# Summing one conditioning vector by TensorE instead of GpSimd, and a wider spacing of the conditioning loads between the first FFN's output weights

## Chip, core and metric

One core of one Trainium2 chip runs the whole program. The metric is device time in microseconds (us). Five engines work in order, each on its own queue: TensorE (PE, matmuls; its weight loads are listed as PEld), VectorE (DVE), ScalarE (ACT), GpSimd (POOL) and SyncE (SP), which here only issues DMAs. They wait for each other by semaphores.

## What is computed

Two transformer layers on 512 tokens of width 1024, in fp32: layer 0 has a gated linear recurrence (HGRN2) as mixer, layer 1 dilated attention; each is followed by a SwiGLU FFN of width 2816. Every layer is conditioned by six vectors of 1024 (shift, scale and gate for mixer and FFN), all from one vector `c`:

```
cond = silu(c)
for layer in range(2):
    mod = cond @ ada_w[layer] + ada_b[layer]
    sh1, sc1, g1, sh2, sc2, g2 = split(mod, 6)
    u = rms_norm(h, norm_g[layer, 0]) * (1 + sc1) + sh1
    y = hgrn2_mixer(u) if layer == 0 else dilated_attention_mixer(u)
    h = h + (1 + g1) * rms_norm(y, norm_g[layer, 1])
    u = rms_norm(h, norm_g[layer, 2]) * (1 + sc2) + sh2
    y = (silu(u @ w_gate) * (u @ w_up)) @ w_out
    h = h + (1 + g2) * rms_norm(y, norm_g[layer, 3])
```

## The kernel before

**Weights.** All weights and all `ada_w` pieces come through one stream (`Stream`, lines 35 to 140): a list `items` in a fixed order, 1 MB or less each, loaded by SP into two buffers `raw` in turn (line 70; the two bias rows of a gate at line 64). A buffer is loaded again when its last reader has done. A weight item is split into two parts for three-pass fp32 matmuls: ACT writes `hi` (line 90), DVE writes `lo = raw - hi` (line 91), and each has three buffers. The helper `three` (lines 575 to 578) issues the three matmuls of a product, hi, lo and the low part of the other operand.

**Conditioning.** A vector (l, v) is made in two halves of 512 columns (hf), each from two loads of 512 rows of `ada_w` (kq). In `ada_chunk` DVE multiplies each 128-row block by its scalar of `cond` and adds it up in an accumulator of 128 x 512 (lines 391 and 393). What is left is the sum over the 128 partitions: for most vectors GpSimd does it (`partition_all_reduce`, line 395), and then `col_fin` turns it into columns with DVE, one masked reduction of 128 x 128 for each of four column blocks (line 405, two instructions each). For the three vectors (0, 2), (0, 3) and (0, 4) the products are made by TensorE (`ada_groups`), and the sum too: `col_fin` multiplies each 128-column block of the accumulator by a column of ones (line 420) into one PSUM bank of tag "b". Either way DVE then adds the bias (line 409) and, for scales, the norm's weight (line 411).

**Order.** `weave` (in `block_kernel`) puts conditioning items between the weights: group n of the others goes in behind weight number first + n * every. The vectors (0, 2), (0, 4), (0, 3) and (1, 4) are woven into the mixer's input weights; (0, 5), (1, 1) and (1, 0) into the first FFN's. Of the eleven output weights of that FFN (`f0b`, two 128-row blocks each), each is used for 48 matmuls of 128 x 512 into all eight PSUM banks; the last two are used together, token block by token block (`mm`), while the norm of the next layer (`Turn`: lines 605 to 680) already begins.

In the mixer (heads in `head_prep` and `core_a` to `core_d`, lines 1496 to 1596) and in the FFN's output products up to the last two weights, a scheduler orders each engine's instructions by estimated times; so the change moves instructions that it doesn't touch. A head's output is normalised with 1/rms by GpSimd (`orr`, line 591) from DVE's `rv` (line 590); DVE scales it into `aT` (line 1588), TensorE transposes that (line 1595), and ACT copies it out (line 1596). GpSimd also makes two decay-weighted copies of each head, `k` (line 1534) and `q` (line 1537).

Of the kernel before, what the change touches and what calls it, by code (L numbers as in the profile page):

```python
# [292 lines left out]
def block_kernel(tc, x, c, positions, ada_w, ada_b, norm_g, hgrn_w_in, lower, hgrn_norm_g, hgrn_w_out,  # L293
# [8 lines left out]
    with ExitStack() as ctx:  # L302
# [7 lines left out]
        def bank(tag):  # L310
            uid[0] += 1
            return psum.tile([P, 512], F32, name=f"ps_{tag}{uid[0]}", tag=tag, bufs={"mm": 4, "a": 2, "b": 2}[tag])

        def fresh(p, shape, tag, bufs=1, dt=F32):
            uid[0] += 1
            return p.tile(shape, dt, name=f"{tag}{uid[0]}", tag=tag, bufs=bufs)
# [39 lines left out]
        def acc_place():  # L356
            turns_of_acc[0] += 1
            return shared[:, 2 + turns_of_acc[0] % 2]

        by_pe = lambda l, v: l == 0 and v in (2, 3, 4)  # L360

        def ada_groups(l, v, hf, kq):


            def run(raw):
                if kq == 0:
                    accs[l, v, hf] = bank("mm")
                ps, r = accs[l, v, hf], V4(raw)
                for k in range(4):
                    j = slice(32 * k, 32 * k + 32)  # L370
                    pe.matmul(ps[j], cond_tiles[:, kq * 4 + k], r[:, k], start=kq == 0, stop=kq == 1,
                              tile_position=(0, 32 * k))
                if kq == 1:
                    accs[l, v, hf] = acc_place()
                    act.copy(accs[l, v, hf], ps)
            return run

        def ada_chunk(l, v, hf, kq):
            if by_pe(l, v):
                return ada_groups(l, v, hf, kq)  # L380

            def run(raw):
                if kq == 0:
                    accs[l, v, hf] = acc_place()
                a = accs[l, v, hf]
                r = V4(raw)
                for k in range(4):
                    kt = kq * 4 + k
                    sc = cond[:, kt:kt + 1]
                    if kt == 0:  # L390
                        dve.tensor_scalar(a, r[:, k], sc, None, op0=OP.mult)
                    else:
                        dve.scalar_tensor_tensor(a, r[:, k], sc, a, op0=OP.mult, op1=OP.add)
                if kq == 1:
                    pool.partition_all_reduce(a, a, P, bass.bass_isa.ReduceOp.add)
            return run

        def ada_item(l, v, hf, kq):
            src = ada_w[l, kq * 512:(kq + 1) * 512, v * D + hf * 512:v * D + (hf + 1) * 512]
            return ("ada", src.rearrange("(k p) n -> p k n", p=P), ada_chunk(l, v, hf, kq), (l, v, hf, kq))  # L400

        def to_col(dst, rows, k):

            jk = fresh(base, [P, P], "diag", 1)
            dve.tensor_tensor_reduce(jk, rows[:, k * P:(k + 1) * P], ident, 1.0, 0.0, OP.mult, OP.add, dst)

        def col_done(l, v, sl, src=None):
            dst = cols[:, l * 4 + v - (1 if v > 2 else 0), sl]
            dve.tensor_add(dst, dst if src is None else src, abc(l, v)[:, sl])
            if v in (1, 4):  # L410
                dve.scalar_tensor_tensor(dst, dst, 1.0, ngc(l, 0 if v == 1 else 2)[:, sl], op0=OP.add, op1=OP.mult)

        def col_fin(l, v, hf):

            def run(_=None):
                a = accs.pop((l, v, hf))
                if by_pe(l, v):
                    b = bank("b")
                    for k in range(4):
                        pe.matmul(b[:, k:k + 1], a[:, k * P:(k + 1) * P], ones[:, 0:1], start=True, stop=True)  # L420
                    col_done(l, v, slice(hf * 4, hf * 4 + 4), b[:, 0:4])
                    return
                for k in range(4):
                    c = l * 4 + v - (1 if v > 2 else 0)
                    to_col(cols[:, c, hf * 4 + k:hf * 4 + k + 1], a, k)
                col_done(l, v, slice(hf * 4, hf * 4 + 4))
            return run

        def row_fin(l, v, hf):

            def run(raw):
                if hf == 0:
                    gates[l, v] = fresh(base, [P, D], "gate", 1)
                g = gates[l, v][:, hf * 512:(hf + 1) * 512]
                a = accs.pop((l, v, hf))
                if by_pe(l, v):
                    b = bank("b")
                    pe.matmul(b, ones, a, start=True, stop=True)
                    a = b
                dve.tensor_add(g, a, raw[:, 0:512])  # L440
                dve.scalar_tensor_tensor(g, g, 1.0, raw[:, 512:D], op0=OP.add, op1=OP.mult)
            return run
# [9 lines left out]
        def ada_seq(*vecs):  # L452

            res, last = [], None
            for l, v in vecs:
                for hf in range(2):
                    res.append([ada_item(l, v, hf, 0)])
                    res.append(([fin_item(*last)] if last else []) + [ada_item(l, v, hf, 1)])
                    last = (l, v, hf)
            return res + [[], [fin_item(*last)]]  # L460
# [15 lines left out]
        def weave(ws, others, first, every=1):  # L476

            res, o, n = [], list(others), 0
            for i, w in enumerate(ws):
                res.append(w)  # L480
                while i >= first + n * every and o:
                    res += o.pop(0)
                    n += 1
            return res + [i for g in o for i in g]

        items = []
# [11 lines left out]
        def ffn_ws(l):  # L498

            a, w = [], ffn_w_in[l]  # L500
            for j in range(PLAIN[l]):
                a += [win(w, j * 256), win(w, DFF + j * 256)]
            for f in range(2 * PLAIN[l], NF):
                a.append(("quarters", tuple(w[:, c:c + P].rearrange("(k p) n -> p k n", p=P) for c in (DFF + f * P, f * P))))
            return a, [wrow(ffn_w_out[l], j) for j in range(NF // 2)]

        items += weave(hg, ada_seq((0, 2), (0, 4), (0, 3), (1, 4)), 1, 0.7) + hg_o
        f0a, f0b = ffn_ws(0)
        n0 = 2 * PLAIN[0]
        gate, gate_fins = ada_halves(0, 5)  # L510
        one, two = ada_seq((1, 1)), ada_seq((1, 0))
        items += weave(f0a[:n0], [one[0], one[1], [], one[3][:1]], 2) + f0a[n0:]
        late = [gate[0], gate[1], gate[2], gate_fins[:1] + gate[3], one[2], gate_fins[1:] + one[3][1:], two[0], one[5] + two[1]]
        items += weave(f0b, late + two[2:], 0, 0.8)
        AW = attn_w_in[0]

        def av(g, hf):
# [30 lines left out]
        late = ada_seq((1, 2), (1, 3))  # L548
# [785 lines left out]
        early, late = slice(0, 256), slice(256, S)  # L1334
# [1040 lines left out]
        for kind, g, i in order:  # L2375
            if kind == "v":
                steps += [("v", None, None, k, *p) for k, p in enumerate(value_unit(g - 1, i))]
            else:
                two = sevens(g, i) if by_seven(g) else plain(g, i)
# [120 lines left out]
```

## Time and profile before

| | |
|---|---|
| time, median of three runs | 1509.28 us (1507.06 to 1509.78) |
| the profiled execution's own time | 1508.73 us |
| its span, first to last instruction | 1507.0 us |
| TensorE: busy, mean granted clock | 98% of the span, 0.993 |
| busy share of DVE, ACT, POOL | 73%, 53%, 13% |
| mean DMA rate | 133 GB/s |
| mixer of layer 0, in this trace | about 90 to 300 us |
| output weights of the first FFN | about 540 to 686 us |

How to read the views: a row of the timeline gives start, duration, engine, line, operation, output<-inputs, and in brackets the idle time of the engine before it and what ended it. Matmuls overlap, so the spacing of their starts is what one costs. In a table by windows, the sixth entry is the granted TensorE clock as a share of the full one (PEclk). Rows of "SPq" are DMAs being issued.

### The profile page before, as it was taken

The page shows a single profiled execution, that of the slowest core. Times are in us where ns is not written, and L with a number is a line of the kernel's source. Part 1 is how long each engine was busy: PE and PEld are TensorE (multiplying, and loading weights), DVE is VectorE, ACT ScalarE, POOL GpSimd, SP SyncE. Part 2 cuts the span into 40 slices and gives each one's busy share as a digit, 9 for nine tenths or more (in the row PEclk, how much of TensorE's full clock was granted, in tenths as well). Part 3 has the DMA queues.
Part 4 walks back from the last instruction along what each step waited for, and adds up shares of the span by engine and source line. Part 5 has one row for each costly group of instructions (what it writes and reads, how often), then busy time and mean ns, then how long its engine had stood idle before and what let it go on. Part 6 is the DMA issues. An engine that isn't in the chain of part 4 may idle for free. (4 is left out here: it accounts for less than half of the span.)

```text
span 1507.0 us, 25055 instructions
## 1 busy us (share of the span) xinstructions
PE 1477.4 (98%) x9807; PEld 1323.1 (88%) x9807; DVE 1096.8 (73%) x1816; ACT 797.3 (53%) x1474; POOL 197.5 (13%) x174
## 2 busy tenths in 40 slices
PE   8999998999999999999999999999999999999998
PEld 6777787888999997788999999999988899999886
DVE  4577677578688876777788877878766978887533
ACT  4433342464455542256637878567875655555231
POOL 1011013031111110222001010001012211110100
PEclk9999999999999999999999999999999999999999
DMA  9554553315333345634234443254343333434531
GB/s 307 179 173 138 184 168 112 112 57 157 93 107 108 107 155 206 226 136 140 82 121 137 131 129 94 81 161 123 91 154 126 97 100 113 113 111 142 199 110 56
DMA packets 210151, 201.09 MB, mean 133 GB/s; under 512 B 8248, under 2 KB 167920, under 8 KB 209776
## 3 DMA queue, kind: packets, MB, share of 16 engines
q1 hardware_dynamic: 207056, 192.71, 40.7%
q10 hardware_dynamic: 1952, 6.65, 1.2%
q8 instruction: 77, 1.26, 0.3%
q0 software_dynamic: 1024, 0.13, 0.2%
q14 instruction: 42, 0.34, 0.1%
HBM read 192.31 MB, written 5.31 MB: 131 GB/s over the span
## 5 line engine op out<-in xcount | busy, mean ns | idle before, releaser
L91 DVE TENSOR_TENSOR lo<-raw,hi 128x2048 fp32r<-128x2048 f32 x43 | 103.2, 2402 | 62.5 <-ACT hi L90 62.4
L90 ACT CAST hi<-raw 128x2048 fp32r<-128x2048 f32 x43 | 82.1, 1909 | 123.6 <-DMA raw<-in_ffn_w_out_dram 51.9
L576 PE MATMUL ps_mm<-uh,hi 128*128 128x512 f32 (+1 forms) x400 | 146.2, 366 | 0.0
L577 PE MATMUL ps_mm<-ul,hi 128*128 128x512 f32 (+1 forms) x400 | 144.8, 362 | 1.0 <-DVE ul L676 1.0
L578 PE MATMUL ps_mm<-uh,lo 128*128 128x512 f32 (+1 forms) x400 | 144.2, 360 | 0.0
L1981 PE MATMUL ps_mm<-apart,hiq 128*128 128x256 f32 (+1 forms) x608 | 142.0, 326 | 0.1
L1981 PEld LDWEIGHTS ps_mm<-apart,hiq 128*128 128x128 f32 x608 | 99.9, 189 | 8.3 <-ACT xs L2095 0.3
L1981 PE MATMUL ps_mm<-apart,loq 128*128 128x256 f32 (+1 forms) x304 | 97.4, 320 | 0.4 <-DVE loq L2117 0.4
L963 PE MATMUL ps_mm<-tl,hiq 128*128 128x256 f32 x340 | 93.9, 276 | 0.0
L963 PE MATMUL ps_mm<-th,loq 128*128 128x256 f32 x340 | 93.9, 276 | 0.0
L963 PE MATMUL ps_mm<-th,hiq 128*128 128x256 f32 x340 | 93.9, 276 | 0.0
L954 DVE TENSOR_TENSOR loq<-raw,hiq 128x1024 fp32r<-128x1024 f32 x68 | 80.3, 1222 | 18.6 <-ACT hiq L950 18.6
L576 PEld LDWEIGHTS ps_mm<-uh,hi 128*128 128x128 f32 x400 | 75.5, 189 | 18.4 <-issue 6.7
L577 PEld LDWEIGHTS ps_mm<-ul,hi 128*128 128x128 f32 x400 | 75.7, 189 | 12.5 <-DVE ul L676 1.4
L578 PEld LDWEIGHTS ps_mm<-uh,lo 128*128 128x128 f32 x400 | 75.5, 189 | 12.6 <-issue 1.1
L576 PE MATMUL ps_mm<-hi,oh 128*128 128x512 f32 x208 | 82.3, 396 | 4.2 <-ACT hi L90 4.2
L934 POOL TENSOR_TENSOR raw<-raw 128x512 f32<-128x512 f32 x34 | 44.8, 1316 | 304.6 <-DVE spare L930 138.6
L577 PE MATMUL ps_mm<-lo,oh 128*128 128x512 f32 x208 | 81.4, 392 | 0.0
L950 ACT CAST hiq<-raw 128x1024 fp32r<-128x1024 f32 x68 | 68.1, 1049 | 17.5 <-DVE raw L938 15.9
L1981 PE MATMUL ps_mm<-uh,hiq 128*128 128x256 f32 x256 | 71.8, 281 | 0.0
L1981 PE MATMUL ps_mm<-ul,hiq 128*128 128x256 f32 x256 | 71.2, 278 | 0.0
L1981 PE MATMUL ps_mm<-uh,loq 128*128 128x256 f32 x256 | 71.2, 278 | 0.0
(479 smaller groups left out, 4636.4 us busy)
## 6 DMA issues: line engine op xcount, KB each, us to landing
raw<-in_ada_w_dram SPq DMA_DIRECT2D x40, 1024.0 KB, 5.0
raw<-in_ffn_w_in_dram SPq DMA_DIRECT2D x136, 256.0 KB, 4.0
raw<-in_ffn_w_out_dram SPq DMA_DIRECT2D x22, 1024.0 KB, 4.8
raw<-in_attn_w_in_dram SPq DMA_DIRECT2D x64, 256.0 KB, 4.6
raw<-in_hgrn_w_in_dram SPq DMA_DIRECT2D x12, 1024.0 KB, 5.3
raw<-in_attn_w_in_dram SPq DMA_DIRECT2D x12, 1024.0 KB, 4.9
raw<-in_ffn_w_in_dram SPq DMA_DIRECT2D x10, 1024.0 KB, 5.0
raw<-in_attn_w_in_dram SPq DMA_DIRECT2D x16, 512.0 KB, 4.9
```

Source lines behind the costliest of these rows:

```text
L90: self.nc.scalar.copy(hi, t)
L91: self.nc.vector.tensor_sub(lo, t, hi.bitcast(F32))
L576: pe.matmul(ps, ah, bh, start=start, stop=False, skip_group_check=part)
L577: pe.matmul(ps, ah, bl, start=False, stop=False, skip_group_check=part)
L578: pe.matmul(ps, al, bh, start=False, stop=stop, skip_group_check=part)
L934: pool.tensor_add(r[:, 2], r[:, 2], r[:, 0])
L950: act.copy(hi, src)
L954: dve.tensor_sub(lo, src, hi.bitcast(F32))
L963: pe.matmul(ps, w[x][:, a], us[kt][y], start=begin and kt + m == 0, stop=kt == 3 and m == 2, skip_group_check=True)
L1981: pe.matmul(dst(), x, y, start=begin and i == 0, stop=i == len(todo) - 1, skip_group_check=True)
```

## The change

A second predicate, `sum_by_pe`, is true for the three vectors that TensorE already made and for (1, 4), the scale of layer 1's FFN. It takes the place of `by_pe` where the sum over partitions is chosen: for (1, 4) GpSimd's `partition_all_reduce` isn't issued, and `col_fin` takes the branch with four matmuls against ones. The products of (1, 4) stay on DVE. And in the weave of the first FFN's output weights, `every` goes from 0.8 to 0.95.

```
-        by_pe = lambda l, v: l == 0 and v in (2, 3, 4)
+        by_pe = lambda l, v, hf: l == 0 and v in (2, 3, 4)
+        sum_by_pe = lambda l, v, hf: by_pe(l, v, hf) or (l, v) == (1, 4)
...
-            if by_pe(l, v):
+            if by_pe(l, v, hf):
                 return ada_groups(l, v, hf, kq)
...
-                if kq == 1:
+                if kq == 1 and not sum_by_pe(l, v, hf):
                     pool.partition_all_reduce(a, a, P, bass.bass_isa.ReduceOp.add)
...
                 a = accs.pop((l, v, hf))
-                if by_pe(l, v):
+                if sum_by_pe(l, v, hf):
                     b = bank("b")
                     for k in range(4):
                         pe.matmul(b[:, k:k + 1], a[:, k * P:(k + 1) * P], ones[:, 0:1], start=True, stop=True)
...
                 a = accs.pop((l, v, hf))
-                if by_pe(l, v):
+                if sum_by_pe(l, v, hf):
                     b = bank("b")
                     pe.matmul(b, ones, a, start=True, stop=True)
                     a = b
...
-        items += weave(f0b, late + two[2:], 0, 0.8)
+        items += weave(f0b, late + two[2:], 0, 0.95)
```

From line 361 on, a line of the changed kernel has a number higher by one.

On GpSimd, in the mixer, the rows before are these (ISA rows without operands switch the code that GpSimd runs):

```order
L591 TENSOR_TENSOR orr_1920<-rv_1921,expo 128x4
L395 ISA
L395 ISA shared<-shared 128x512
L1537 ISA
L1537 TENSOR_TENSOR q_2063<-qd_2041,fpre_2047 128x512
L591 TENSOR_TENSOR orr_1994<-rv_1995,expo 128x4
```

In the changed kernel the same place reads:

```order
L592 TENSOR_TENSOR orr_1920<-rv_1921,expo 128x4
L1538 TENSOR_TENSOR q_2063<-qd_2041,fpre_2047 128x512
L592 TENSOR_TENSOR orr_1994<-rv_1995,expo 128x4
L1535 TENSOR_TENSOR k_2173<-T_1902,fsuf_2157 128x512
L1538 TENSOR_TENSOR q_2172<-qd_2150,fpre_2156 128x512
```

The all-reduce and the two switches around it are gone; the same happens once more, two instructions later, for the second half of the vector.

On TensorE, in the same stretch, the transposes of a head (`aT_1988`) stand before the change between two triples of a gate's products (`ps_mm_2187`):

```order
L576 MATMUL ps_mm_2187<-uh,hi_1809 128x512
L577 MATMUL ps_mm_2187<-ul,hi_1809 128x512
L578 MATMUL ps_mm_2187<-uh,lo_1810 128x512
L1595 MATMUL ps_a_2027<-ident,aT_1988 128x128 x4
L576 MATMUL ps_mm_2187<-uh,hi_1809 128x512
```

In the changed kernel (that bank is `ps_mm_2179` there):

```order
L577 MATMUL ps_mm_2179<-uh,hi_1809 128x512
L421 MATMUL ps_b_2088<-ones,shared 128x1 x4
L1596 MATMUL ps_a_2027<-ident,aT_1988 128x128 x4
L578 MATMUL ps_mm_2179<-ul,hi_1809 128x512
```

The four transposes come eleven matmuls earlier, behind the first new group of four matmuls against ones. The second new group stands later, among the small products of the next head (line 1548).

On SP, in the first FFN's output weights, the loads from the sixth weight on stand so before (`ada_w` pieces, the two bias rows of a gate, and weights):

```order
L70 DMA raw_5318<-in_ada_w_dram 128x4x512
L64 DMA raw_5324<-in_ada_b_dram 128x512
L64 DMA raw_5324<-in_norm_g_dram 128x512
L70 DMA raw_5387<-in_ada_w_dram 128x4x512
L70 DMA raw_5391<-in_ffn_w_out_dram 128x2x1024
L70 DMA raw_5398<-in_ada_w_dram 128x4x512
L70 DMA raw_5404<-in_ffn_w_out_dram 128x2x1024
```

And in the changed kernel:

```order
L70 DMA raw_5310<-in_ada_w_dram 128x4x512
L70 DMA raw_5316<-in_ffn_w_out_dram 128x2x1024
L64 DMA raw_5378<-in_ada_b_dram 128x512
L64 DMA raw_5378<-in_norm_g_dram 128x512
L70 DMA raw_5385<-in_ada_w_dram 128x4x512
L70 DMA raw_5445<-in_ffn_w_out_dram 128x2x1024
L70 DMA raw_5452<-in_ada_w_dram 128x4x512
```

The sixth weight is loaded ahead of the bias rows and of one conditioning piece; from there to the end, one weight and one conditioning piece alternate, and the eleventh weight comes behind the last conditioning piece, where before it followed the tenth directly. With it TensorE's order changes in three of the weights (the sixth, seventh and eighth): before, the eight `hi` matmuls (seven in one case) of a weight's first block come ahead of all `lo` matmuls; in the changed kernel each bank takes its three matmuls in a row, so that `lo` is needed one matmul after `hi`.

More of the change, by code (lines that the diff above doesn't have):

```diff
@@ L358, in acc_place @@
             return shared[:, 2 + turns_of_acc[0] % 2]
-        by_pe = lambda l, v: l == 0 and v in (2, 3, 4)
+        by_pe = lambda l, v, hf: l == 0 and v in (2, 3, 4)
+        sum_by_pe = lambda l, v, hf: by_pe(l, v, hf) or (l, v) == (1, 4)
         def ada_groups(l, v, hf, kq):
@@ L378, in ada_chunk @@
         def ada_chunk(l, v, hf, kq):
-            if by_pe(l, v):
+            if by_pe(l, v, hf):
                 return ada_groups(l, v, hf, kq)
@@ L393, in run @@
                         dve.scalar_tensor_tensor(a, r[:, k], sc, a, op0=OP.mult, op1=OP.add)
-                if kq == 1:
+                if kq == 1 and not sum_by_pe(l, v, hf):
                     pool.partition_all_reduce(a, a, P, bass.bass_isa.ReduceOp.add)
@@ L416, in run @@
                 a = accs.pop((l, v, hf))
-                if by_pe(l, v):
+                if sum_by_pe(l, v, hf):
                     b = bank("b")
@@ L435, in run @@
                 a = accs.pop((l, v, hf))
-                if by_pe(l, v):
+                if sum_by_pe(l, v, hf):
                     b = bank("b")
@@ L513, in block_kernel @@
         late = [gate[0], gate[1], gate[2], gate_fins[:1] + gate[3], one[2], gate_fins[1:] + one[3][1:], two[0], one[5] + two[1]]
-        items += weave(f0b, late + two[2:], 0, 0.8)
+        items += weave(f0b, late + two[2:], 0, 0.95)
         AW = attn_w_in[0]
```

## Prediction

> **What bounds the kernel now.** I read the page's busy times first, then TensorE's waits, then the timeline around the two longest. The page:
>
> ```profile
> PE 1477.4 (98%) x9807; PEld 1323.1 (88%) x9807; DVE 1096.8 (73%) x1816; ACT 797.3 (53%) x1474; POOL 197.5 (13%) x174
> ```
>
> TensorE is busy for 98% of the span, so only its work and its pauses can change the time. Who it waited for (total, times, longest), the two longest of all:
>
> ```profile
> PE ps_a L1595 <- DVE aT L1588: 6.3, 2, 4.8
> PE ps_mm L576 <- ACT hi L90: 4.2, 1, 4.2
> ```
>
> The first lies in the mixer (place H). On TensorE's timeline:
>
> ```profile
> 245.32 0.39 PE L577 MATMUL ps_mm<-ul,hi 128*128 128x512 f32 x1
> 245.55 0.39 PE L578 MATMUL ps_mm<-uh,lo 128*128 128x512 f32 x1
> 250.69 0.71 PE L1595 MATMUL ps_a<-ident,aT 128*128 128x128 f32 x4 [4.76 <-DVE aT L1588]
> 251.08 0.75 PE L576 MATMUL ps_mm<-uh,hi 128*128 128x512 f32 x1
> 254.82 0.40 PE L576 MATMUL ps_mm<-uh,hi 128*128 128x512 f32 x1
> ```
>
> A 128x512 matmul costs 0.23 us, start to start. After the wait nine of them take 254.82 - 251.08 = 3.74 us, 0.42 each. The windows (sixth entry is the clock) say why, here and after the other wait:
>
> ```profile
> 251.00:255.00 4.00, 4.00 (x13) 3.21 (x12) 4.00 (x9) 0.69 (x1) 1.31 (x1) 0.57 0.00 0
> 604.00:609.00 5.00, 5.00 (x12) 3.48 (x13) 5.00 (x8) 0.22 (x1) 2.26 (x1) 0.50 0.77 227
> ```
>
> So a long wait is paid twice: idle, then some 4 to 5 us at about half the clock. Without the wait, 254.82 would be 245.55 + 0.23 + 0.39 (transposes) + 9 x 0.23 + 0.1 (change of operation) = 248.3: place H loses **6.5 us**.
>
> Who held it up is on GpSimd's and DVE's timelines:
>
> ```profile
> 237.39 3.25 POOL L395 PARTITION_ALL_REDUCE shared<-shared  x1 [7.64 <-DVE ki L1509]
> 247.76 1.04 POOL L1537 TENSOR_TENSOR q<-qd,fpre 128x512 f32<-128x512 f32 x1 [7.12 <-issue]
> 248.77 1.05 POOL L591 TENSOR_TENSOR orr<-rv,expo 128x4 f32<-128x4 f32 x1
> 249.85 0.69 DVE L1588 TENSOR_TENSOR aT<-ps_b,orr 128x512 f32<-128x512 f32 x1 [4.85 <-POOL orr L591]
> ```
>
> The transposes wait for `aT`, that for `orr`, and `orr` stands in GpSimd's queue behind the all-reduce of (1, 4). The all-reduce takes 3.25 us, but a pause of 7.64 us lies ahead of it and one of 7.12 us, in which nothing was waited for, behind it: the switches of code. It is these 14.8 us that hold the queue.
>
> The second wait (place F) is in the first FFN's output weights:
>
> ```profile
> 599.16 0.39 PE L578 MATMUL ps_b<-hi,ol 128*128 128x512 f32 x1
> 603.75 0.79 PE L576 MATMUL ps_mm<-hi,oh 128*128 128x512 f32 x1 [4.21 <-ACT hi L90]
> 609.89 0.40 PE L577 MATMUL ps_b<-lo,oh 128*128 128x512 f32 x1
> 588.66 0.34 SPq L64 DMA_DIRECT2D raw<-in_ada_b_dram  x1
> 594.17 0.38 SPq L70 DMA_DIRECT2D raw<-in_ada_w_dram  x1
> 594.83 0.38 SPq L70 DMA_DIRECT2D raw<-in_ffn_w_out_dram  x1
> 601.80 1.90 ACT L90 CAST hi<-raw 128x2048 fp32r<-128x2048 f32 x1 [7.26 <-DMA raw<-in_ffn_w_out_dram]
> ```
>
> From 599.16 to 609.89 are 15 starts, worth 3.4 us at 0.227: place F loses **7.3 us**. The sixth weight was issued only at 594.83; the buffer that came free at 588.66 went to the bias rows, and the next one to another conditioning piece.
>
> **The change at place H.** Added: two groups of four matmuls against ones. One such group stands in the trace already:
>
> ```profile
> 236.67 0.95 PE L420 MATMUL ps_b<-ones,shared 128*128 128x1 f32 x8
> 237.48 0.48 PE L576 MATMUL ps_mm<-uh,hi 128*128 128x512 f32 x1
> ```
>
> It takes 237.48 - 236.67 = 0.81 us of TensorE; two cost 1.6 us, and nothing hides them. Removed: both all-reduces with their switches, and DVE's 16 instructions of line 405, replaced by the bias add alone. Neither GpSimd's nor DVE's work counts by itself; what counts is when `aT` is ready. The rows for that:
>
> ```profile
> 233.52 3.34 DVE L1509 RECIPROCAL ki<-bb 128x512 f32<-128x512 f32 x1
> 240.67 0.29 DVE L405 CUSTOM_DVE_ANT_0 diag<-shared,ident 128x128 f32<-128x128 f32 x1 [3.81 <-POOL shared L395]
> 244.32 0.69 DVE L1511 TENSOR_TENSOR qd<-bb,Q 128x512 f32<-128x512 f32 x1
> 242.37 0.39 PE L576 MATMUL ps_mm<-uh,hi 128*128 128x512 f32 x1
> ```
>
> The reciprocal ends at 236.86, where DVE stood 3.81 us for the all-reduce. What lies between that and `aT` took until 244.32 + 0.69 = 245.0, 4.3 us; so in the changed kernel it ends by 241.2, and `aT` (0.69) by 241.9. `orr` isn't later: its `rv` stands among those DVE instructions, and GpSimd needs 1.04 + 1.05 us for `q` and `orr`. TensorE comes to the new group behind 22 matmuls from 237.48, at 242.37 + 0.23 = 242.6, and to the transposes 0.81 later. The margin is 0.7 us at the new group (its PSUM bank is one that `aT` reads) and 1.5 at the transposes: the wait goes, and the half clock with it. Net at H: 6.5 - 1.6 = **4.9 us**. If the cover of 0.7 us is gone, each us late costs one. The second group waits for the accumulator's last products. DVE has twelve instructions for it behind `aT`, up to 0.7 us each (about 6.7 us in all, an estimate from the rows above: 248.6); TensorE has the group, the transposes, 20 matmuls and four small products of the next head ahead of it, about 6.9 us from 242.6 (249.5): no wait, or a few tenths.
>
> The Trainium skill, GPSIMD Engine Reference, section 4.1 Engine selection, names GpSimd for reducing along the partition dimension, which speaks against this edit. By it the sum should stay on GpSimd, and H would gain nothing; the trace disagrees, with 0.81 us against 3.25 plus the switches.
>
> **The change at place F.** The sixth weight takes the buffer at 588.66. The rows that time what follows:
>
> ```profile
> 592.18 0.69 DVE L440 TENSOR_TENSOR gate<-shared,raw 128x512 f32<-128x512 f32 x1 [0.93 <-DMA raw<-in_ada_b_dram]
> 603.73 3.68 DVE L91 TENSOR_TENSOR lo<-raw,hi 128x2048 fp32r<-128x2048 f32 x1 [0.80 <-ACT hi L90]
> 614.63 2.29 DVE L91 TENSOR_TENSOR lo<-raw,hi 128x2048 fp32r<-128x2048 f32 x1 [1.12 <-ACT hi L90]
> 616.95 0.37 SPq L70 DMA_DIRECT2D raw<-in_ffn_w_out_dram  x1
> 625.95 0.37 SPq L70 DMA_DIRECT2D raw<-in_ffn_w_out_dram  x1
> 621.68 1.91 ACT L90 CAST hi<-raw 128x2048 fp32r<-128x2048 f32 x1 [3.45 <-DMA raw<-in_ffn_w_out_dram]
> 653.22 0.39 PE L577 MATMUL ps_mm<-lo,oh 128*128 128x512 f32 x1
> ```
>
> A weight lands 4.7 us after its issue (616.95 to 621.68), so the sixth is there by 594 and its `hi` by 596. Ahead of its `lo` DVE has to add the bias rows, now issued some 4 us later, at about 592.5; they need 3.5 us (588.66 to 592.18): 596.0, then 0.6 for the add and 2.3 for `lo`: 598.9. TensorE asks for it at 599.6. The 7.3 us go, but two smaller waits come, because the loads now run one buffer turn behind each other to the end. The seventh weight is issued beside a conditioning piece at 599.6, as 594.83 was beside 594.17, and takes the same 7.0 us: 606.6. `hi` to 608.5; `lo` lies beside an all-reduce, as the row of 3.68 us did, and takes about 3.4: 611.9, where TensorE wants it at 610.5. **Wait of 1.4 us.** Then each turn is 9.0 us (616.95 to 625.95): the `lo` of the eighth to eleventh weights at 620.9, 629.9, 639.0 and 648.0, give or take 0.3. TensorE takes 48 x 0.227 = 10.9 us a weight and gains on them, but the last two weights are used together: the eleventh's `lo` is wanted 13 matmuls into the tenth, at 599.4 + 1.4 + 4 x 10.9 + 2.9 = 647.3. **Wait of 0.9 us**, to 648.2. Before, that matmul started at 653.22 (the last row). Net at F: **5.0 us**, bounded by 7.3 if both new waits vanish, and by 0 if the chain of loads slips.
>
> **Sum.** 4.9 + 5.0 = 9.9 us; less a tenth for norm work that starts nearer to TensorE: 9.8. The profiled execution took 1508.73 us (span 1507.0); 1508.73 - 9.8 = **1498.9 us**. The median before is 0.55 above that execution; I leave it in the range. Everything later is TensorE-bound with waits of 1.3 us at most, so the gain isn't given back there.
>
> **Rivals.** *Both places clean*: 4.9 + 7.3, so 1496.5. For it: my 3.4 us for `lo` and 7.0 for the load come from pairs that may fall apart. *New waits cost clock too*:
>
> ```profile
> 151.86 0.85 PE L1595 MATMUL ps_a<-ident,aT 128*128 128x128 f32 x4 [1.56 <-DVE aT L1588]
> 152.00:156.00 4.00, 4.00 (x38) 3.64 (x38) 1.33 (x5) 0.69 (x1) 0.00 (x0) 0.57 0.76 281
> ```
>
> A wait of 1.56 us, behind a group against ones, was followed by 4 us at 0.57, so 1.7 us lost. If either new wait does that, 0.8 to 1.7 us go, 2.5 for both: about 1500.9. The Trainium skill (TensorE: Matmul & The Clock Gate, "What's actually happening") has the clock fall after an idle window of about 3.4 us. By that rule waits of 1.4 and 0.9 cost no clock and the sum stays; the row at 152 shows a fall after 1.56, so I keep the rival. *One place only*: 1508.73 - 4.9 = 1503.8 if the wait at F merely moves; 1505.3 if H keeps its wait and adds the 1.6. Against it: the margins above. *Slower*: the loads at F slip by one buffer turn, 9.0 us, say because the bias rows land late and the seventh weight with them. GpSimd's last all-reduce then ends nearer to the norm:
>
> ```profile
> 638.74 3.23 POOL L395 PARTITION_ALL_REDUCE shared<-shared  x1 [14.99 <-DVE shared L393]
> 656.94 0.60 POOL L627 TENSOR_TENSOR rr<-rv,expo 128x1 f32<-128x1 f32 x1 [14.97 <-DVE rv L625]
> 660.72 0.76 DVE L651 TENSOR_SCALAR xn<-h,rr 128x1024 f32<-128x1024 f32 x1 [0.67 <-POOL rr L627]
> 663.88 0.60 PE L657 MATMUL ps_mm<-ident,xn 128*128 128x128 f32 x4
> ```
>
> Before it ended at 641.97 with 15 us to spare for the switch of 7.1. By my times it ends at 646; a turn later, 655.1 + 7.1 = 662.2 for `rr`, which is 6.9 us ahead of the transposes at 663.88: 669.1, so 5.2 late, with two falls of the clock, 2.3 us each (H and F lost 1.6 and 3.0 beyond their idle time). 1508.73 - 4.9 + 5.2 + 4.6 = 1513.6. It decides only if the loads slip by about 6 us or more.
>
> **Chances.** Forecast 0.52, both clean 0.15, clock 0.16, one place 0.09, in between (two halves lost) 0.04, slower 0.04. The range, 1495.0 to 1504.5, takes in the first three and "one place" but for 1505.3, and 1.5 us at the low end for the spread of the runs (1507.06 to 1509.78). Over 0.2% (3 us, about what a measurement of this kernel can tell from no change) faster: the first four but 0.02 of "one place", 0.90; within: 0.06; slower: 0.04.
>
> **What would show it.** H is right if no wait stands ahead of line 1596, the clock there stays at 1, and GpSimd's `q` and `orr` follow `rv` at once. F is right if the sixth weight's `hi` starts near 594 (less the 4.9 of H), and TensorE waits only for `lo` of the seventh and of the eleventh weight. A wait for `ps_b` at line 421, or a clock below 1 after 611 or 648, would make it wrong.

## The result, and the profile after

The changed kernel takes 1503.27 us (median of 5 runs, 1500.42 to 1505.12) beside 1509.78 for the kernel before on the same chip: ratio 0.9952, 95% interval 0.9940 to 0.9964, so 7.2 us faster (5.4 to 9.1). Two repeats gave 0.9955 (0.9942 to 0.9968) and 0.9962 (0.9948 to 0.9976): 6.8 and 5.7 us. The prediction said 9.8 us: right in its sign and its range, 2.6 to 4 us too much in size.

The profiled execution took 1504.35 us (span 1502.6). Its page, and TensorE's longest waits (total, times, longest):

```profile
PE 1476.8 (98%) x9823; PEld 1323.5 (88%) x9823; DVE 1095.8 (73%) x1800; ACT 797.2 (53%) x1474; POOL 191.3 (13%) x172
```

```profile
PE ps_a L2321 <- ACT h L2306: 2.7, 1, 2.7
PE ps_mm L578 <- DVE lo L91: 2.4, 2, 1.8
PE ps_a L1596 <- DVE aT L1589: 1.6, 1, 1.6
```

Both waits that the prediction started from are gone. Two waits for `lo` in the FFN's output weights are new, and the longest now stands at line 2321, the end of attention, where 0.7 us stood before.

**Place H** on the timeline of the changed kernel, GpSimd, DVE and TensorE:

```profile
236.90 1.01 POOL L592 TENSOR_TENSOR orr<-rv,expo 128x4 f32<-128x4 f32 x1 [4.64 <-DVE rv L591]
239.87 0.68 DVE L1589 TENSOR_TENSOR aT<-ps_b,orr 128x512 f32<-128x512 f32 x1
241.15 0.95 PE L421 MATMUL ps_b<-ones,shared 128*128 128x1 f32 x8
241.96 0.63 PE L1596 MATMUL ps_a<-ident,aT 128*128 128x128 f32 x4
```

`orr` now waits for its own input `rv` and for nothing else, `aT` is ready at 240.55, and TensorE goes from the new group into the transposes without a pause. The windows there (length, TensorE's busy time and instructions, clock, DMA share, GB/s):

```profile
236.00:243.00 7.00, 7.00 (x39) 1.00 0.00 0
248.00:253.00 5.00, 5.00 (x50) 1.00 0.68 240
```

**Place F**, the `lo` of the seventh weight with the all-reduce beside it, that of the eleventh, and TensorE's two waits for them:

```profile
602.76 3.60 DVE L91 TENSOR_TENSOR lo<-raw,hi 128x2048 fp32r<-128x2048 f32 x1 [0.89 <-ACT hi L90]
601.97 3.23 POOL L396 PARTITION_ALL_REDUCE shared<-shared  x1 [20.06 <-DVE shared L394]
641.89 2.29 DVE L91 TENSOR_TENSOR lo<-raw,hi 128x2048 fp32r<-128x2048 f32 x1 [3.58 <-ACT hi L90]
606.41 0.50 PE L578 MATMUL ps_mm<-lo,oh 128*128 128x512 f32 x1 [1.84 <-DVE lo L91]
644.24 0.51 PE L578 MATMUL ps_mm<-lo,oh 128*128 128x512 f32 x1 [0.57 <-DVE lo L91]
```

```profile
606.00:610.00 4.00, 3.59 (x10) 0.66 0.68 226
610.00:614.00 4.00, 4.00 (x17) 0.92 0.79 263
```

The waits are the two that the prediction named, with a fall of the clock to 0.66 behind the first that it had kept for a rival.

Single spans mislead here, since two executions of one kernel differ by several us at places that the change doesn't touch. So I compare stretches of TensorE's program from one instruction to the same one in the other kernel. In the mixer the stretch runs from the last transposes of `aT` ahead of place H (TensorE, line 1595 or 1596) to the second such group behind them. First of the kernel before, then of the changed one:

```profile
233.96 0.38 PE L1595 MATMUL ps_a<-ident,aT 128*128 128x128 f32 x2
282.48 0.38 PE L1595 MATMUL ps_a<-ident,aT 128*128 128x128 f32 x2
```

```profile
231.83 0.38 PE L1596 MATMUL ps_a<-ident,aT 128*128 128x128 f32 x2
275.82 0.38 PE L1596 MATMUL ps_a<-ident,aT 128*128 128x128 f32 x2
```

It shrank from 48.52 to 43.99 us. In the FFN it runs from the first matmul of the first output weight to the 492nd, the last ahead of the norm's transposes:

```profile
544.96 0.40 PE L576 MATMUL ps_mm<-hi,oh 128*128 128x512 f32 x1
663.64 0.40 PE L578 MATMUL ps_a<-hi,ol 128*128 128x512 f32 x1
```

```profile
538.85 0.40 PE L577 MATMUL ps_mm<-hi,oh 128*128 128x512 f32 x1
654.84 0.40 PE L579 MATMUL ps_a<-hi,ol 128*128 128x512 f32 x1
```

That is 118.68 and 115.99 us, where 491 starts at 0.227 are worth 111.5. The two stretches give 4.5 and 2.7, together the 7.2 us of the timed runs. Here are all profiles of this study; "11th" is the end of the eleventh weight's `lo`, counted from the FFN stretch's first matmul (641.89 + 2.29 - 538.85 = 105.33 for the rows above), "wait" that at the end of attention, and "clock" that of the 4 us behind it:

```
kernel                          ratio, 95% interval        mixer   FFN     11th    wait   clock
before                          1                          48.52   118.68  102.91  0.71   1.00
before, second profile          -                          48.25   119.18  105.00  3.53   0.59
changed                         0.9952 (0.9940 to 0.9964)  43.99   115.99  105.33  2.72   0.68
changed, second profile         0.9955 (0.9942 to 0.9968)  43.99   116.84  106.21  1.33   0.73
changed, third profile          0.9962 (0.9948 to 0.9976)  43.99   116.20  105.54  4.04   0.50
sum by TensorE alone            0.9979 (0.9965 to 0.9993)  43.99   119.86  105.93  2.37   0.65
loads further apart alone       0.9990 (0.9976 to 1.0004)  48.93   115.09  104.45  0.97   1.00
changed, one all-reduce out     0.9965 (0.9950 to 0.9980)  43.99   114.76  104.16  3.07   0.76
changed, unread sum             single run                 52.97   116.79  106.17  1.40   1.00
changed, unread sum, 4 columns  single run                 49.68   118.28  106.03  0.68   1.00
changed, a piece early          0.9929 (0.9915 to 0.9943)  43.99   112.49   99.50  1.17   1.00
the same, second profile        0.9934 (0.9919 to 0.9949)  43.99   112.73  102.12  1.62   1.00
a piece early, old spacing      0.9935 (0.9921 to 0.9949)  43.99   112.41   94.57  1.50   1.00
changed, a piece later          0.9986 (0.9976 to 0.9996)  43.99   112.63  101.97  1.06   0.72
```

### The profile page after: what moved, and what is told of

The parts are those of the page before. It is cut to its first block, busy times and chain, and to the rows that moved or that the text cites. A ratio compares the mean times of both kernels' runs of the same rounds, so it can differ in the third digit from the quotient of the medians.

```text
span 1502.6 us, 25061 instructions
## 1 busy us (share of the span) xinstructions
PE 1476.8 (98%) x9823; PEld 1323.5 (88%) x9823; DVE 1095.8 (73%) x1800; ACT 797.2 (53%) x1474; POOL 191.3 (13%) x172
```

## The experiments

**The parts alone.** The first is the changed kernel with one number put back, the second the kernel before with that number alone changed:

```
-        items += weave(f0b, late + two[2:], 0, 0.95)
+        items += weave(f0b, late + two[2:], 0, 0.8)
```

> Only the sum of (1, 4) by TensorE; the loads as before. Theory (the two edits act in two places and add up, place H is worth its forecast): no wait at line 1596, full clock there, 4.5 to 4.9 us faster than the kernel before; the 4.2 us wait for `hi` in the FFN's output weights stays with its fall of the clock. Rival (H's gain is partly given back at line 2321, as in the first profile of the changed kernel): a wait there of over 2 us and only 1 to 2 us gained.

> Only the loads further apart; the sum of (1, 4) stays on GpSimd. By the prediction's term F: 5.0 us faster. By the first profile of the changed kernel, where the new waits of 1.84 and 0.57 us were followed by a clock of 0.62 to 0.94: 2.5 to 3.2 us faster, with these waits and this clock again, and the wait of 4.8 us at line 1595 unchanged. Rival (the loads were not what held TensorE there): within 1 us of the kernel before.

The sum alone: ratio 0.9979, so 3.2 us (1.1 to 5.3), less than the 4.5 that the mixer's stretch shows. The FFN's stretch is 119.86, 0.7 to 1.2 longer than in the kernel before (118.68 and 119.18). The sixth weight's issue and TensorE's wait there:

```profile
591.49 0.38 SPq L70 DMA_DIRECT2D raw<-in_ffn_w_out_dram  x1
600.49 0.79 PE L577 MATMUL ps_mm<-hi,oh 128*128 128x512 f32 x1 [5.38 <-ACT hi L90]
```

The wait is 5.38 us; the two profiles of the kernel before have 4.21 and 4.83. The second of them has this weight issued as late as here, 50.96 us behind the stretch's first matmul, so the lateness needs no edit, and it isn't shown that the sum by TensorE costs anything in the FFN with the old spacing. The loads alone: 0.9990, 1.5 us (-0.6 to 3.6), where the stretch shows 3.6 to 4.1, at the edge of the interval; the first wait is 1.81 us with the clock at 0.57 behind it, the second doesn't come. The rival that the loads didn't matter falls by the stretch, not by the time. Alone the edits give 4.7 us, together 6.8; the intervals are too wide to say that they help each other.

**What held `orr`.** GpSimd makes its sum of (1, 4) after all, from the same products and at the same place, into a tile that nobody reads (a free part of `shared`; in the second kernel a tile of 4 columns, and the sum of 4 columns only):

```
+        unread = shared[:, 1]
...
+                if kq == 1 and (l, v) == (1, 4):
+                    pool.partition_all_reduce(unread, a, P, bass.bass_isa.ReduceOp.add)
```

> The changed kernel, but GpSimd still makes its sum of (1, 4) from the same products at the same place, into a tile that nobody reads; TensorE's sum is the one used. Theory Q (GpSimd's queue was what held TensorE: switch, all-reduce, switch, and `orr` behind them): `orr` and `aT` as late as in the kernel before, a wait of about 4 us at line 1596 again (4.76 less the 0.8 of TensorE's own sum), the clock near 0.57 behind it, and nearly all of place H's gain gone: 5 to 6 us slower than the changed kernel. Rival D (DVE held it: its 3.81 us of waiting for the all-reduce and the 16 instructions of line 405): no wait at line 1596, and the changed kernel's time.

> As the one before, but the unread all-reduce takes 4 columns in place of 512. Theory Q with the switches of code as the price (7.64 and 7.12 us, against 3.25 for the sum itself): the switches stay and only the sum shrinks, by 2 us or so; a wait of about 2 us stays at line 1596. If the sum itself were the price: GpSimd's `q` and `orr` follow within 1 us and no wait is left.

With the full unread sum:

```profile
235.62 3.71 POOL L399 PARTITION_ALL_REDUCE shared<-shared  x1 [7.49 <-DVE f L1533]
247.15 1.04 POOL L1541 TENSOR_TENSOR q<-qd,fpre 128x512 f32<-128x512 f32 x1 [7.83 <-issue]
248.16 1.05 POOL L595 TENSOR_TENSOR orr<-rv,expo 128x4 f32<-128x4 f32 x1
250.08 1.09 PE L1599 MATMUL ps_a<-ident,aT 128*128 128x128 f32 x4 [7.52 <-DVE aT L1592]
```

With 4 columns:

```profile
235.94 0.84 POOL L399 PARTITION_ALL_REDUCE unread<-shared  x1 [7.66 <-PE ps_b L424]
243.66 1.04 POOL L1541 TENSOR_TENSOR q<-qd,fpre 128x512 f32<-128x512 f32 x1 [6.88 <-issue]
246.59 1.09 PE L1599 MATMUL ps_a<-ident,aT 128*128 128x128 f32 x4 [4.09 <-DVE aT L1592]
```

No consumer needs these sums, and TensorE waits all the same: it is GpSimd's queue. The wait shrinks by 3.4 us when the sum shrinks by 2.9, and 4.1 us are left with almost no sum: the pauses of about 7 us ahead and behind stay, whatever the size. Both waits are longer than expected, by 3.5 and 2, mostly because in the changed order 11 of the 0.23 us matmuls that stood ahead of the transposes now stand behind them, which I had not counted: TensorE is there at 242.5. In this order a held queue costs 9.0 us of the mixer's stretch (52.97 for 43.99), more than in the kernel before.

**What sets place F.** First, the all-reduce that lay over the seventh `lo` taken out:

```
-                if kq == 1 and not sum_by_pe(l, v, hf):
+                if kq == 1 and not sum_by_pe(l, v, hf) and (l, v, hf) != (1, 1, 1):
```

> The changed kernel without GpSimd's sum over partitions for the second half of (1, 1): that vector is left unsummed, so the output is not the reference's. In the changed kernel this all-reduce (601.97 to 605.20) lies over `lo` of the seventh output weight, which takes 3.60 us in place of 2.29. Theory (the wait of 1.84 us at line 578 is made of the late load and of this overlap, and the clock falls because of the wait): `lo` takes 2.29, the wait falls to about 0.5, the clock there stays at 1, and 2 to 3 us are gained on the changed kernel. Rival (`lo` is slow for another reason, say the loads beside it): `lo` stays at 3.6 and the time within 0.5 us of the changed kernel.

```profile
603.83 2.29 DVE L91 TENSOR_TENSOR lo<-raw,hi 128x2048 fp32r<-128x2048 f32 x1
606.17 0.50 PE L578 MATMUL ps_mm<-lo,oh 128*128 128x512 f32 x1 [0.86 <-DVE lo L91]
```

`lo` takes 2.29 us again and the wait falls to 0.86, with the clock at 1.00. But TensorE, earlier now, waits 1.82 us for the eleventh weight instead of 0.57: the idle time is moved, not removed. The stretch is only 1.2 us shorter than the changed kernel's shortest, by just what the eleventh `lo` is earlier (104.16 for 105.33), and the time shows nothing (0.9965 beside 0.9955).

This is the key to the table. The stretch less "11th" is 10.60 to 10.66 us in every kernel with the new spacing, but for the one with 4 columns (12.25, the clock at 0.62 behind its wait for the eleventh weight) and the early piece's first profile. (With the loads alone TensorE came to the eleventh `lo` 0.2 us after it was ready, so there the sum agrees without a wait, and the 3.6 us are the first wait and its clock.) It makes no difference whether the clock fell behind the first wait (the changed kernel, three times) or stayed at 1.00 behind 2.23 us (the unread sum, 116.79): in the changed kernel the eleventh weight sets the end, and what TensorE loses ahead of it only shortens its last wait. The end of a weight's `lo` frees the buffer for the next weight, so these issues follow each other (changed kernel, eighth to eleventh weight):

```profile
606.39 0.37 SPq L70 DMA_DIRECT2D raw<-in_ffn_w_out_dram  x1
615.63 0.37 SPq L70 DMA_DIRECT2D raw<-in_ffn_w_out_dram  x1
625.47 0.37 SPq L70 DMA_DIRECT2D raw<-in_ffn_w_out_dram  x1
634.75 0.37 SPq L70 DMA_DIRECT2D raw<-in_ffn_w_out_dram  x1
```

606.39 is the end of the seventh `lo` (602.76 + 3.60), and each turn takes 9.2 to 9.8 us. ACT's rows for the ninth weight, in the changed kernel's first and second profile, show what differs:

```profile
621.21 1.91 ACT L90 CAST hi<-raw 128x2048 fp32r<-128x2048 f32 x1 [6.90 <-DMA raw<-in_ffn_w_out_dram]
623.27 1.91 ACT L90 CAST hi<-raw 128x2048 fp32r<-128x2048 f32 x1 [7.67 <-DMA raw<-in_ffn_w_out_dram]
```

From the start of `hi` to the next issue are 4.3 us each time (625.47 - 621.21); the rest of a turn is the load. The ninth weight's took 5.58 us in the first profile (621.21 - 615.63) and 6.36 in the second; the eighth's, tenth's and eleventh's took 4.9 to 5.2. A long load of the ninth weight, 5.6 to 6.4 us, stands in all eight profiles with the sum by TensorE and without the early piece of the next experiment, and 4.8 to 5.1 in the six others. Why is open; but it is the largest part of why the loads alone, with 5.09, have a stretch 0.9 to 1.8 us shorter than the change.

Then the chain of loads itself: one piece moved from behind the first output weight into the plain part of the FFN. Its partial sums are kept in the gate's own tile from then on.

```
-        items += weave(f0a[:n0], [one[0], one[1], [], one[3][:1]], 2) + f0a[n0:]
-        late = [gate[0], gate[1], ...
+        items += weave(f0a[:n0], [one[0], one[1], gate[0], one[3][:1]], 2) + f0a[n0:]
+        late = [[], gate[1], ...
...
-                if kq == 0:
+                if kq == 0 and (l, v, hf) == (0, 5, 0):
+                    gates[l, v] = fresh(base, [P, D], "gate", 1)
+                    accs[l, v, hf] = gates[l, v][:, 0:512]
+                elif kq == 0:
```

> The changed kernel with one conditioning load (first piece of the FFN's gate) moved from behind the first output weight into the plain part of the first FFN, with its partial sums kept in the gate's own tile. Theory C (place F is bound by the chain of loads over two buffers: a weight is issued when the one before it has been split, so each 1 MB ahead of it delays the whole chain): the second and third output weights are issued 10 us or more earlier, TensorE waits neither for `lo` of the seventh nor of the eleventh weight, the clock there stays at 1, and 2.5 to 4 us are gained on the changed kernel, near the 1496.5 of the prediction's first rival on its scale. Rival (the pair of bias rows and piece behind the sixth weight makes the wait by itself, however early the chain begins): a wait of over 1 us for the seventh weight stays, gain under 1 us.

> The kernel with the early piece once more, beside the changed kernel on the same chip. Its first run: ratio 0.9929, no wait and full clock in the FFN's output weights. If that stands: again about 0.993, 3 to 4 us under the changed kernel of this call. If it was chance (the small transfers at line 2321 cost 1 to 4 us from one execution to the next): within 1.5 us of it.

The ratio is 0.9929 and in the repeat 0.9934, beside 0.9962 for the changed kernel on the same chip: 10.7 and 10.0 us faster than before, the most that any version here gained. TensorE over place F, in the first profile:

```profile
600.00:610.00 10.00, 10.00 (x45) 1.00 0.62 218
610.00:640.00 30.00, 30.00 (x134) 1.00 0.61 210
```

No pause and full clock; of the stretch only 1.0 us over 111.5 is left, and the eleventh `lo` is ready 5.8 us earlier than in the changed kernel's first profile. One number of the expectation was off: counted from the stretch's first matmul, the third weight goes out 6.9 us earlier (543.40 - 540.82 beside 548.32 - 538.85) and the sixth 8.1 (577.02 beside 583.10, by the same), not 10. It is enough.

With the early piece and the old spacing of 0.8:

> The early piece, the sum by TensorE, and the old spacing of 0.8. Theory C: what counts is when the sixth weight can be issued; with the chain begun about 5 us earlier than in the kernel with the sum alone (there issued at 591.5, wait 5.4 us), it goes out near 586.5 and TensorE waits 0.5 to 2 us for it, so most of the gain is kept: 1 to 4 us slower than the early piece with the new spacing. Rival (the spacing itself decides, the early piece is worth little without it): the wait of 4 to 5 us stays, and the time is that of the sum alone (ratio near 0.998).

```profile
579.92 0.38 SPq L70 DMA_DIRECT2D raw<-in_ffn_w_out_dram  x1
```

The ratio is 0.9935, the same as with the new spacing, and TensorE doesn't wait for any weight. My theory was right in kind and wrong in its number: counted from the first matmul, the sixth weight goes out 10.5 us earlier than with the sum alone (579.92 - 539.45 beside 591.49 - 540.52), not 5. So the spacing shows no worth of its own once the chain of loads has a lead (the intervals leave 2 us either way); it repairs the late sixth weight, and so does the lead.

Last, the opposite: the piece behind the sixth weight, and each later one, put off by a weight.

```
-        late = [..., one[2], gate_fins[1:] + one[3][1:], two[0], ...
+        late = [..., one[2], gate_fins[1:], one[3][1:], two[0], ...
```

> The changed kernel with the conditioning piece behind the sixth weight put off until behind the seventh, and each later piece with it. Theory C (chain of loads): the seventh weight goes out half a us earlier and its `lo` no longer lies beside an all-reduce, so its wait falls from 1.84 us to under 1, with the clock at 1. But the prediction's last rival now has its condition: the last all-reduce ends one turn (9.3 us) later, near 651, with 7.1 us of switch behind it, so `rr` comes near 658 instead of 649.2, and TensorE waits some 5 us ahead of line 658, with a fall of the clock: 5 to 7 us lost, 1 to 2.5 gained, 3 to 6 us slower than the changed kernel. If the pieces had a turn to spare there (against that rival): no such wait, and 1 to 2.5 us faster than the changed kernel.

```profile
644.22 3.23 POOL L396 PARTITION_ALL_REDUCE shared<-shared  x1 [15.23 <-DVE shared L394]
654.42 0.59 POOL L628 TENSOR_TENSOR rr<-rv,expo 128x1 f32<-128x1 f32 x1 [6.97 <-issue]
658.19 0.76 DVE L652 TENSOR_SCALAR xn<-h,rr 128x1024 f32<-128x1024 f32 x1 [0.67 <-POOL rr L628]
659.00 1.11 PE L658 MATMUL ps_mm<-ident,xn 128*128 128x128 f32 x4 [7.33 <-DVE xn L652]
```

The seventh weight's wait is gone (0.8 us for the eleventh is all), and the prediction's last rival is there in its place: the last all-reduce ends at 647.45, the switch of 6.97 follows, `rr` starts with no wait but the switch, and TensorE stands 7.33 us. The ratio is 0.9986, 3.6 us slower than the changed kernel. That rival was real; the change just stayed clear of it. There `rr` ran 7.58 us behind the last all-reduce, and waited for its input:

```profile
649.22 0.60 POOL L628 TENSOR_TENSOR rr<-rv,expo 128x1 f32<-128x1 f32 x1 [7.58 <-DVE rv L626]
```

**Repeats, for the end of attention.** The kernels unaltered:

> The changed kernel unaltered, profiled a second time. In its first profile TensorE waited 2.72 us at line 2321 (end of attention) and then ran at 0.68 of its clock, where the kernel before waited 0.71 at full clock; on DVE's row the small transfer `so` landed 5.33 us after its issue (1110.09 to 1115.42), not 3.60. Theory J (the give-back is a chance delay of that one small transfer): the second profile shows about 3.6 us, a wait of at most 1.3 us and a span near 1498.6. Theory S (systematic: TensorE is earlier, so the transfer meets other traffic or the chain of small transfers is the bound): again over 5 us, a wait of 2 to 3 us and a span of 1502 to 1503. Gain by the timed rounds 6.5 to 7.5 us under either, as before.

> The kernel before, unaltered, profiled a second time, to see what at the end of attention belongs to the change. So far TensorE waited there (line 2320 before, 2321 after) 0.71 us in the kernel before, 0.97 with the loads alone, 1.33 and 2.72 with both edits, 2.37 with the sum alone; from the issue of the first small transfer `scr<-so` to DVE's use of the last took 13.92, 14.19, 14.55, 15.93 and 15.60 us. Theory J (chance: small transfers beside two loads of 1 MB): this profile can show 1 to 3 us as well, and a chain of 14 to 16 us. Theory S (the sum by TensorE brings it): again about 0.7 us and 13.9 us.

> The changed kernel, as the measure for the others of this call: a ratio of 0.995 to 0.996. Waits of 1.8 to 2.0 us for `lo` of the seventh weight and 0.6 to 1.1 for the eleventh, clock 0.6 to 0.8 behind the first; at line 2321 anything from 0.7 to 3.5 us, as in the profiles so far.

The second profile of the kernel before: issue of the last small transfer, DVE's use of it, TensorE's wait, and the clock behind it.

```profile
1117.34 0.76 POOL L2288 DMA_DIRECT2D so<-scr  x1 [3.24 <-DMA scr<-so]
1122.92 0.17 DVE L2297 TENSOR_TENSOR wM<-so 128x8 f32<-128x8 f32 x1 [5.37 <-DMA so<-scr]
1125.28 0.33 PE L2320 MATMUL ps_a<-ident,h 128*128 128x128 f32 x1 [3.53 <-ACT h L2305]
```

```profile
1125.30:1129.30 4.00, 3.86 (x12) 0.59 0.00 0
```

The same of the changed kernel's first profile:

```profile
1110.09 0.76 POOL L2289 DMA_DIRECT2D so<-scr  x1 [3.03 <-DMA scr<-so]
1115.42 0.17 DVE L2298 TENSOR_TENSOR wM<-so 128x8 f32<-128x8 f32 x1 [4.59 <-DMA so<-scr]
1117.77 2.30 PE L2321 MATMUL ps_a<-ident,h 128*128 128x128 f32 x8 [2.72 <-ACT h L2306]
```

The transfer of 4 KB is used 5.58 and 5.33 us after its issue, and 3.60 in the first profile of the kernel before. Over all 14 profiles it is 3.60 to 5.75 and the wait 0.7 to 4.0: 0.71 and 3.53 in the kernel before, 1.33 to 4.04 in the changed one, and 0.68 and 1.06 in two variants that have the sum by TensorE. Theory S falls: it had the kernel before again near 0.7. The 3.5 us that the first two profiles put there (TensorE's instructions come 7.9 us earlier than in the kernel before ahead of that place, and 4.4 us earlier after it) are within what one kernel does by chance, not shown to be any part of the change.

## Why the prediction was right or wrong

**H: right.** No wait at line 1596, clock 1, `orr` at once behind `rv`, as it said. The stretch gives 4.3 to 4.5 us, forecast 4.9; the first new group costs 0.81 us (241.15 to 241.96), as forecast. The unread sums show the mechanism: the queue with its switches, not DVE.

**F: right in the mechanism, wrong in the size.** The step that failed is "Then each turn is 9.0 us (616.95 to 625.95)", and with it "Net at F: **5.0 us**". The loss before stood at 7.3 and is 7.2 and 7.7 by the stretch. The two new waits stood at 1.4 and 0.9 and are there. But the forecast had the eleventh `lo` at 648.0 and TensorE going on at 648.2, which is 103.2 us behind the stretch's first matmul (544.96), and it is ready at 105.3, 106.2 and 105.5: 2.1 to 3.0 us late, and late by that is the whole stretch. Net 2.6 on average. The lateness has two parts: the seventh `lo` ends 67.5 to 67.9 us behind the first matmul (forecast 611.9, so 66.9), and the four turns to the eleventh take 37.8 to 38.4 us where I put 36.1. I had read the length of a turn from one pair of issues, and it was the shortest of the three that the kernel before shows (607.44 to 616.95 is 9.5, 625.95 to 635.10 is 9.2). The term in it that was too small is the load: 4.7 us (616.95 to 621.68) for each weight, where the eighth's, tenth's and eleventh's took 4.9 to 5.2 and the ninth's 5.6 to 6.4; what follows a load took 4.3 us in both kernels. The mean of the three turns would have given 36.9 us for four, still 0.9 to 1.5 short: no row of the kernel before shows the long load.

**The rival "New waits cost clock too"** looks like the winner, and isn't. The falls came (0.61, 0.60 and 0.58 in the 4 us behind the first wait in the three profiles of the changed kernel), worth some 2 us; but in the unread sum, where none came, the stretch was as long, since the eleventh weight was no earlier. Its price was hidden, and the same two us were lost in the last wait.

The clock also doesn't follow the wait's length alone. In the changed kernel's first profile:

```profile
151.25 0.52 PE L1596 MATMUL ps_a<-ident,aT 128*128 128x128 f32 x3 [1.58 <-DVE aT L1589]
```

```profile
152.00:156.00 4.00, 4.00 (x46) 1.00 0.66 248
```

At this instruction, where the prediction had its row of 1.56 us and 0.57, all 14 profiles show a wait of 1.54 to 1.67 us; the clock fell behind it in 6 and stayed at 1.00 in 8. Behind the 15 waits from 2.37 us up it always fell. The Trainium skill (TensorE: Matmul & The Clock Gate, "What's actually happening") says that the window over which activity is watched is free-running, so that the moment of a change depends on where in it the work lands. If that holds for a pause too, the 6 and 8 agree with it. The same section has the slow clock come after an idle window of about 3.4 us; here it came behind waits of 1.06 to 2.15 us, so that length is not what this kernel shows.

**"So the gain isn't given back there"** was right, though the first pair of profiles seemed to say the opposite: spans 4.4 us apart, where the two stretches give 7.2. The end of attention took back some 3.5 us, and the clock behind 151 us gave some 1.7, both as chance alone can.

**Rivals.** Both clean: not in this kernel, but nearly so with the early piece. One place only: no, each part alone shortens the stretch at its own place. Slower: it didn't come; its mechanism was shown by putting the piece off. (Its price for a fall of the clock, 1.6 and 3.0 us, is 1.7 and 3.1 by the prediction's own rows, 6.5 - 4.76 and 7.3 - 4.21; that would move this rival's 1513.6 by 0.2.)

## What to carry to other kernels

Price an operation that makes GpSimd change its code by what stands behind it in the queue: here 0.84 us of work held TensorE for 4.1. Where loads run through two buffers, follow the chain to its last link and take the turn from all turns shown, since the last link sets the end and hides what was lost ahead of it; one load moved out of the chain brought more than spreading the rest. And profile both kernels twice before explaining a few us at a place that the change doesn't touch.

## What was not expected of the hardware

- The pauses around an all-reduce hardly depend on its size: 7.49 and 7.83 us around 512 columns, 7.66 and 6.88 around 4.
- Waits of the same length at the same instruction cost some 1.7 us of clock in one execution and nothing in the next (6 and 8 of 14).
- DVE's split of a weight takes 2.29 us alone and 3.60 beside an all-reduce of 3.23, so it is slowed and not stopped.
- A transfer of 4 KB through memory, issued at the same point beside the same two loads of 1 MB, took 3.60 to 5.75 us to its use. What makes the difference is open; it was not tried to move it away from these loads.
